# Row sums of a 64 MiB array: handing rows to the partitions at an odd distance, 111 rows in place of 112

## Chip, cores, metric

One core of a Trainium2 chip. The metric is device time in microseconds, the median of several runs.

## The reference

```python
batch, seq, dim = 32, 512, 1024
x = randn(batch, seq, dim)  as float32          # 16384 rows of 4 KiB
def reference(x, multiplier=0.5):
    return (np.sum(x, axis=-1) * multiplier).astype(np.float32)
```

67.11 MB are read, 64 KiB are written. The kernel can hardly be anything but a stream of loads with the sums beside it.

## The kernel before

Of each partition's 128 rows the first 112 are contiguous in HBM (partition p owns rows from 112p). They come in seven loads of 16 rows, 64 KiB per partition, into three buffers. The last 16 rows per partition come from the end of the array in five small pieces, so that little work is left after the last byte. VectorE sums whole blocks; ScalarE helps in the last two. The first three loads are issued ahead of the program's entry barrier.

```python
    own = rows - B                                  # 128 - 16 = 112
    x_rows = x_flat[0 : P * own, :].rearrange("(p c) d -> p c d", p=P)
    x_last = x_flat[P * own : N, :].rearrange("(p c) d -> p c d", p=P)
    x_pool = ctx.enter_context(tc.tile_pool(name="x", bufs=3))
    # ... cut ...
    for b in range(n_blocks - 1):
        c0 = b * B
        t = x_pool.tile([P, B, D], fp32, name="xb")
        loads.append(nc.sync.dma_start(out=t, in_=x_rows[:, c0 : c0 + B, :]))
        h = B if b < n_blocks - 2 else B // 2
        nc.vector.reduce_sum(out=sums[:, c0 : c0 + h], in_=t[:, 0:h, :], axis=mybir.AxisListType.X)
        # ... times mul; rows h to B on ScalarE ...
    t = x_pool.tile([P, B, D], fp32, name="xb")
    for lo, hi in [(0, 8), (8, 13), (13, 15)]:      # then row 15 in two parts
        loads.append(nc.sync.dma_start(out=t[:, lo:hi, :], in_=x_last[:, lo:hi, :]))
    early = nc.sync.dma_start(out=out_rows, in_=res[:, 0:own])
    # ... cut: row by row on VectorE and ScalarE, the last store ...
```

Of the kernel before, what the change touches and what calls it, by code (L numbers as in the profile page):

```python
# [1 line left out]

# [4 lines left out]


@with_exitstack
def kernel(  # L10
    ctx: ExitStack,
    tc: tile.TileContext,
    x: bass.AP,
    multiplier: float,
    out: bass.AP,
):










    nc = tc.nc
    P = nc.NUM_PARTITIONS
    fp32 = mybir.dt.float32
    ADD = mybir.AluOpType.add  # L30

    x_flat = x.flatten_outer_dims()
    N, D = x_flat.shape
    rows = N // P
    out_flat = out.rearrange("b s -> (b s)")
    mul = float(multiplier)

    B = 16
    n_blocks = rows // B
    assert N == P * rows and rows == n_blocks * B  # L40
    own = rows - B
    x_rows = x_flat[0 : P * own, :].rearrange("(p c) d -> p c d", p=P)
    x_last = x_flat[P * own : N, :].rearrange("(p c) d -> p c d", p=P)
    out_rows = out_flat[0 : P * own].rearrange("(p c) -> p c", p=P)
    out_last = out_flat[P * own : N].rearrange("(p c) -> p c", p=P)

    x_pool = ctx.enter_context(tc.tile_pool(name="x", bufs=3))
    res_pool = ctx.enter_context(tc.tile_pool(name="res", bufs=1))
    sums = res_pool.tile([P, rows], fp32, name="sums")
    res = res_pool.tile([P, rows], fp32, name="res")  # L50
    part = res_pool.tile([P, 1], fp32, name="part")

    SYNC = mybir.DependencyInfo(mybir.DependencyClass.Sync, mybir.DependencyReason.DATA)
    ORDER = mybir.DependencyInfo(
        mybir.DependencyClass.NoSync, mybir.DependencyReason.SCHED_ONLY
    )

    def nop_after(engine, waits_for, follows):
        i = engine.nop()
        for w in waits_for:  # L60
            tc.add_manual_dep(i.ins, w.ins.name, SYNC, reason="end seen here")
        for f in follows:
            tc.add_manual_dep(i.ins, f.ins.name, ORDER, reason="in this order")
        return i

    loads = []
    acts = []

    def act_row(t, r, col):
        acts.append(nc.scalar.activation(  # L70
            out=t[:, r, :],
            in_=t[:, r, :],
            func=mybir.ActivationFunctionType.Copy,
            scale=mul,
            accum_out=res[:, col : col + 1],
        ))

    def dve_span(t, r, lo, hi, dst, start=0.0):
        mid = (lo + hi) // 2
        return nc.vector.tensor_tensor_reduce(  # L80
            out=t[:, r, lo:mid],
            in0=t[:, r, lo:mid],
            in1=t[:, r, mid:hi],
            scale=mul,
            scalar=start,
            op0=ADD,
            op1=ADD,
            accum_out=dst,
        )

    for b in range(n_blocks - 1):
        c0 = b * B
        t = x_pool.tile([P, B, D], fp32, name="xb")
        loads.append(nc.sync.dma_start(out=t, in_=x_rows[:, c0 : c0 + B, :]))  # L94
        h = B if b < n_blocks - 2 else B // 2
        nc.vector.reduce_sum(  # L96
            out=sums[:, c0 : c0 + h], in_=t[:, 0:h, :], axis=mybir.AxisListType.X
        )
        nc.vector.tensor_single_scalar(  # L99
            out=res[:, c0 : c0 + h],  # L100
            in_=sums[:, c0 : c0 + h],
            scalar=mul,
            op=mybir.AluOpType.mult,
        )
        for r in range(h, B):
            act_row(t, r, c0 + r)

    c0 = (n_blocks - 1) * B
    t = x_pool.tile([P, B, D], fp32, name="xb")
    cut = 576  # L110
    pieces = [(0, 8), (8, 13), (13, 15)]
    for lo, hi in pieces:
        loads.append(
            nc.sync.dma_start(  # L114
                out=t[:, lo:hi, :], in_=x_last[:, lo:hi, :]
            )
        )
    for lo, hi in ((0, cut), (cut, D)):
        loads.append(
            nc.sync.dma_start(  # L120
                out=t[:, B - 1, lo:hi], in_=x_last[:, B - 1, lo:hi]
            )
        )
    early = nc.sync.dma_start(out=out_rows, in_=res[:, 0:own])
    on_act = {4, 5, 6, 7, 11, 12, 14}
    for r in range(B - 1):
        if r in on_act:
            act_row(t, r, c0 + r)
        else:
            dve_span(t, r, 0, D, res[:, c0 + r : c0 + r + 1])  # L130
    first = dve_span(t, B - 1, 0, cut, part)
    part_seen = nop_after(nc.vector, [first], [])
    final = dve_span(t, B - 1, cut, D, res[:, rows - 1 : rows], start=part)

    tc.add_manual_dep(final.ins, part_seen.ins.name, ORDER, reason="in this order")
    tc.declare_no_dep(final.ins, first.ins.name, reason="waited for by the nop in front")




    seen = nop_after(nc.sync, loads[-8:] + acts[-1:], [])
    store = nc.sync.dma_start(out=out_last, in_=res[:, own:])
    tc.add_manual_dep(store.ins, seen.ins.name, ORDER, reason="in this order")
    for a in acts[-len(on_act) :]:
        tc.declare_no_dep(store.ins, a.ins.name, reason="waited for by the nop in front")
    nop_after(nc.sync, [early, final], [store])

    def start_loads_at_entry(nc_):



        entry, *rest = nc_.main_func.blocks
        is_sp = lambda i: i.engine == mybir.EngineType.SP
        is_load = lambda i: type(i).__name__ == "InstDMACopy"
        for block in rest:
            body = list(block.instructions)
            own = [i for i in body if is_sp(i)]
            if not any(is_load(i) for i in own):
                continue
            lead = []  # L160
            for i in own:
                if not is_load(i) or i.sync_info.on_wait:
                    break
                lead.append(i)
            names = {i.name for i in lead}
            block.instructions = [i for i in body if i.name not in names]
            head = list(entry.instructions)
            at = next(
                k for k, i in enumerate(head) if is_sp(i) and type(i).__name__ == "InstDrain"
            )  # L170
            entry.instructions = head[:at] + lead + head[at:]
            return

    nc.at_finalize(start_loads_at_entry)


# [1 line left out]
_INS = ['x', 'multiplier']  # L178
_OUTS = [((32, 512), 'float32')]

_NUMBERS = {'multiplier': 0.5}


# [26 lines left out]
```

## Time and profile before

| | before |
|---|---|
| time, median of 3 runs | 162.09 us (161.96 to 162.16) |
| span of the profile | 160.2 us |
| DMA packets' share of the span | 97.4% |
| VectorE busy | 119.3 us |
| first block landed | 21.78 us |
| one block of 8 MiB in the stream | 19.35 us |

How to read it: a load has landed when what waits for its data is released; the landings given are the starts of the reductions. The time from one landing to the next is the stream's own pace. VectorE is faster than that, so whatever moves the end must act on the first landing, on the pace, or on the tail. The lines for this are in the prediction.

### The profile page before, as it was taken

To read this page: it belongs to the slowest core of one execution; us is meant where nothing else is said; L and a number is where in the kernel's file an instruction comes from. 1 tells how busy PE (TensorE), PEld (TensorE's weight loads), DVE (VectorE), ACT (ScalarE), POOL (GpSimd) and SP (SyncE) were. 2 spreads that over 40 slices of the span, in tenths; PEclk is the share of its full clock that TensorE was granted. 3 is DMA by queue.
4 is the path that set the end of the run, shared out by engine and by line. 5 is a ranking of instruction groups with operands and counts; after the bars stand their busy time and mean duration, and the time that the engine had idled before them with its cause. 6 is when DMAs were issued, how large, how long until landed. Compare 5 with 4: busy or idle time off the path is not lost.

```text
span 160.2 us, 138 instructions
## 1 busy us (share of the span) xinstructions
DVE 119.3 (74%) x34; ACT 17.3 (11%) x31; POOL 0.2 (0%) x4
## 2 busy tenths in 40 slices
DVE  0000059997799969999599995999959999597443
ACT  0000000000000000000000000000000000599952
POOL 0000000000000000000000000000000000000000
DMA  7996996996996996997997998979969969999992
GB/s 278 507 524 262 524 524 262 524 524 262 524 524 262 524 524 262 524 475 311 524 442 344 524 409 376 524 311 475 524 278 507 524 278 507 393 393 425 430 399 72
DMA packets 2016, 67.18 MB, mean 419 GB/s; under 512 B 480, under 2 KB 608, under 8 KB 736
## 3 DMA queue, kind: packets, MB, share of 16 engines
q1 hardware_dynamic: 2016, 67.18, 97.4%
HBM read 67.11 MB, written 0.07 MB: 419 GB/s over the span
## 4 chain that ended last, share of the span: by engine, by line
DMA 75%; DVE 22%; SPq 1%; issue 0%; DVEq 0%
DMA xb<-in_x_dram 75%; DVE sums L96 22%; SPq L114 1%; DVE xb L80 0%; SPq L120 0%; SPq L94 0%; DVE res L99 0%; DVEq L205 0%
## 5 line engine op out<-in xcount | busy, mean ns | idle before, releaser
L96 DVE TENSOR_REDUCE sums<-xb 128x16 f32<-128x16384 f32 (+1 forms) x7 | 112.0, 16001 | 33.3 <-DMA xb<-in_x_dram 33.3
L70 ACT ACT_TABLE_LOAD x1 | 1.3, 1283 | 137.9 <-DMA xb<-in_x_dram 137.9
L70 ACT ACTIVATE xb<-xb 128x1024 f32<-128x1024 f32 x15 | 15.7, 1045 | 2.1 <-DMA xb<-in_x_dram 2.1
L80 DVE CUSTOM_DVE_ANT_0 xb<-xb 128x512 f32<-128x512 f32 (+1 forms) x9 | 5.6, 664 | 5.0 <-DMA xb<-in_x_dram 5.0
L70 ACT ACTIVATION_READ_ACCUMULATOR xb<-xb 128x1 f32 x15 | 2.8, 187 | 0.0
L99 DVE TENSOR_SCALAR res<-sums 128x16 f32<-128x16 f32 (+1 forms) x7 | 1.2, 174 | 0.2
L80 DVE DVE_READ_ACCUMULATOR2_ANT res<- 128x1 f32 x9 | 0.7, 83 | 0.0
L80 DVE CUSTOM_DVE_ANT_0 xb<-xb,part 128x224 f32<-128x224 f32 x1 | 0.5, 450 | 0.2 <-DMA xb<-in_x_dram 0.2
L191 POOL MEMSET const-bfloat16-1.0<- 128x1 bf16 x1 | 0.1, 101 | 0.0
L191 POOL MEMSET const-uint8-127<- 128x1 uint8 x1 | 0.1, 101 | 0.0
L191 POOL MEMSET const-float32-0.0<- 128x1 f32 x1 | 0.1, 98 | 0.2 <-issue 0.2
L191 POOL MEMSET const-float32-1.0<- 128x1 f32 x1 | 0.1, 98 | 0.0
L80 DVE DVE_READ_ACCUMULATOR2_ANT part<- 128x1 f32 x1 | 0.1, 83 | 0.0
## 6 DMA issues: line engine op xcount, KB each, us to landing
xb<-in_x_dram SPq DMA_DIRECT2D x1, 4096.0 KB, 31.1
xb<-in_x_dram SPq DMA_DIRECT2D x1, 2560.0 KB, 36.9
xb<-in_x_dram SPq DMA_DIRECT2D x1, 1024.0 KB, 38.9
xb<-in_x_dram SPq DMA_DIRECT2D x1, 288.0 KB, 39.1
xb<-in_x_dram SPq DMA_DIRECT2D x1, 224.0 KB, 39.2
xb<-in_x_dram SPq DMA_DIRECT2D x7, 40.8
out_dram<-res SPq DMA_DIRECT2D x1, 56.0 KB, 10.0
out_dram<-res SPq DMA_DIRECT2D x1, 8.0 KB, 1.4
```

The lines of the kernel that those rows point to most:

```text
L70: acts.append(nc.scalar.activation(out=t[:, r, :], in_=t[:, r, :], func=mybir.ActivationFunctionType.Copy, scale=mul, accum_out=res[:, col ...
L80: return nc.vector.tensor_tensor_reduce(out=t[:, r, lo:mid], in0=t[:, r, lo:mid], in1=t[:, r, mid:hi], scale=mul, scalar=start, op0=ADD, o ...
L96: nc.vector.reduce_sum(out=sums[:, c0 : c0 + h], in_=t[:, 0:h, :], axis=mybir.AxisListType.X)
L99: nc.vector.tensor_single_scalar(out=res[:, c0 : c0 + h], in_=sums[:, c0 : c0 + h], scalar=mul, op=mybir.AluOpType.mult,)
L114: nc.sync.dma_start(out=t[:, lo:hi, :], in_=x_last[:, lo:hi, :])
L191: nc = _bacc.Bacc("TRN2", target_bir_lowering=False, num_devices=1)
```

## The change

Intent: partition 4a+b owns 111 rows from row 111(32b+a). If each engine of a load serves groups of four neighbouring partitions, the first reads of neighbouring groups then lie 111 rows apart, an odd number of 4 KiB rows, in place of 4 x 112 = 448 rows, and do not share their low address bits. With 111 rows per partition the blocks become 15 and 6 x 16 rows, and 17 rows are left for the end; the last of them gets a tile of its own (t_end), as the block's tile holds 16.

```diff
-    own = rows - B
-    x_rows = x_flat[0 : P * own, :].rearrange("(p c) d -> p c d", p=P)
+    own = rows - B - 1
+    Q = 4
+    x_rows = x_flat[0 : P * own, :].rearrange("(b a c) d -> a b c d", b=Q, c=own)
 ... (the same for out_rows)
+    c0 = 0
     for b in range(n_blocks - 1):
-        c0 = b * B
+        n = B if b else B - 1
-        loads.append(nc.sync.dma_start(out=t, in_=x_rows[:, c0 : c0 + B, :]))
+        loads.append(nc.sync.dma_start(out=t[:, 0:n, :], in_=x_rows[:, :, c0 : c0 + n, :]))
 ... 
+    t_end = res_pool.tile([P, 1, D], fp32, name="xe")
-    pieces = [(0, 8), (8, 13), (13, 15)]
+    pieces = [(0, 9), (9, 14), (14, B)]
 ... (the last row, in two parts, goes to t_end)
-    on_act = {4, 5, 6, 7, 11, 12, 14}
+    on_act = {5, 6, 7, 8, 12, 13, 15}
```

Note that the source of a load has one dimension more now (32 x 4 partitions with two different steps). I call this the split source, and the old form the plain source.

## The prediction

> **What bounds the kernel now.** I read the page first, then the chain that ended last in order of time, then the DMA bytes in stretches cut at the landings of the blocks, then the first microseconds and the tail in fine stretches. The busy shares and the chain:
>
> ```profile
> DVE 119.3 (74%) x34; ACT 17.3 (11%) x31; POOL 0.2 (0%) x4
> q1 hardware_dynamic: 2016, 67.18, 97.4%
> DMA 75%; DVE 22%; SPq 1%; issue 0%; DVEq 0%
> ...
> L96 DVE TENSOR_REDUCE sums<-xb 128x16 f32<-128x16384 f32 (+1 forms) x7 | 112.0, 16001 | 33.3 <-DMA xb<-in_x_dram 33.3
> ```
>
> VectorE waits 33.3 us for data and is busy 74%; the DMA engines' packets fill 97.4% of the span. The 22% of VectorE in the chain is no bound: it comes in where a load waits for its buffer, and the queue holds the next load by then. The stretches from one block's landing to the next show that (columns: stretch in us from the start and its length, busy us of VectorE, ScalarE and GpSimd, granted clock, DMA share, GB/s):
>
> ```profile
> 21.78:41.11 19.33, 17.39 (x2) 0.00 (x0) 0.00 (x0) 1.00 1.00 434
> 60.46:79.81 19.35, 17.39 (x3) 0.00 (x0) 0.00 (x0) 1.00 1.00 434
> 99.16:118.51 19.35, 17.39 (x2) 0.00 (x0) 0.00 (x0) 1.00 1.00 434
> 137.87:157.47 19.60, 14.48 (x20) 17.32 (x31) 0.00 (x0) 1.00 0.95 404
> 157.47:160.20 2.73, 0.46 (x2) 0.00 (x0) 0.00 (x0) 1.00 0.03 3
> ```
>
> An 8 MiB block takes 19.35 us, 8,388,608 B / 19.35 us = 433.5 GB/s, with the engines full. VectorE needs 17.39 us of each, so it has 2 us of slack. (A packet is counted where it starts, so the rows near the end read a little low; 8 MiB in the last 19.60 us is 428 GB/s.) The span is 21.78 (first landing) + 6 x 19.35 + 19.60 + 2.73 = 160.2 us. Only three places differ from the steady stream: the first block (21.78 - 19.35 = 2.43 us more), the last one (0.25 us more) and the tail of 2.73 us.
>
> The start, in tenths of a microsecond and then whole waves of 16 packets (64 KiB each, 16 x 65,536 B = 1.05 MB, which GB/s times the length of the stretch confirms):
>
> ```profile
> 1.00:1.10 0.10, 0.00 (x0) 0.00 (x0) 0.00 (x0) 1.00 7.84 2621
> 1.80:1.90 0.10, 0.00 (x0) 0.00 (x0) 0.00 (x0) 1.00 4.67 1966
> ...
> 1.00:1.95 0.95, 0.00 (x0) 0.00 (x0) 0.00 (x0) 1.00 3.03 1104
> 3.90:4.55 0.65, 0.00 (x0) 0.00 (x0) 0.00 (x0) 1.00 3.72 1613
> 8.75:9.40 0.65, 0.00 (x0) 0.00 (x0) 0.00 (x0) 1.00 3.72 1613
> ```
>
> The share counts a packet whole in the stretch where it starts, so share times length is the mean time of the wave's 16 packets: 3.03 x 0.95 = 2.88 us in the first wave, 3.72 x 0.65 = 2.42 us in the second and the fourth. In the first wave the four packets that start in 1.00 to 1.10 took 7.84 x 0.1 x 16 / 4 = 3.14 us each, the three that start in 1.80 to 1.90 took 4.67 x 0.1 x 16 / 3 = 2.49 us. So engines start over 0.9 us, the early ones are held up by about 0.7 us, and all end at nearly one time: the second wave begins within 3.90 to 4.55. After that every wave has the 2.42 us of a full stream.
>
> **What the Trainium skill says.** "DMA: Bandwidth & Descriptors", section "Latency and other measured facts", reports that HBM copies fall to half their rate when the row pitch of the partitions is a large power of two, and that 4 KiB of padding restores it; it calls the aliasing of channels an inference. Here a partition's pitch is 112 rows of 4 KiB, 448 KiB, and four partitions lie 7 x 256 KiB apart, so aliasing would fit the change's intent. The trace shows no such loss in the stream: 433.5 GB/s. The same page, section "Where 436 GB/s comes from", gives 435.2 GB/s as the ceiling of the 16 ports; the trace agrees, it stands at 99.6% of it. "The descriptor swizzle" there says that each engine of a 128-partition transfer writes one port, in groups of four neighbouring partitions, which is why the change hands out rows by 4a+b; this trace does not name engines, so it cannot confirm that.
>
> **The change part by part.**
> 1. *Rows per partition.* In lockstep the 16 engines now read 448 rows (1.75 MiB) apart, with the same low 18 address bits. Afterwards their first reads lie 111 rows or multiples apart, with different low bits. Bytes stay 67.11 MB, descriptors stay 128 per load and 64 KiB long (60 KiB in the first block). What it can remove is the hold-up of the first wave only. Mean excess is 2.88 - 2.42 = 0.46 us per engine, but the end is set by the last engine, and the late starters are the ones hardly held up: one that starts at 1.88 (the stretches place the last start just before 1.90) would end at 4.30, and the last of the second wave's starts is near 4.50. So about 0.2 us of the 0.46 can reach the end. I book it whole: -0.2 us.
> 2. *The stream.* If the odd distance also lifts 433.5 to the port ceiling of 435.2, 67.11 MB would take 154.2 in place of 154.8 us: -0.6 us at most. Nothing in the trace says that HBM is what costs the 0.4%; booked at 0.
> 3. *Block sizes.* One row of all partitions is 512 KiB, 524,288 B / 433.5 GB/s = 1.21 us. Block 0 lands 1.21 us earlier, its reduction takes 17.22 x 15/16 = 16.1 us, and all landings up to the seventh block's come 1.21 us earlier; the last 17 rows give that back. Sum 0.
> 4. *The last pieces.* The first piece has 9 rows instead of 8, five on VectorE (its rows start 0.61 us apart) and four on ScalarE (1.04 us apart). VectorE has the seventh block's half done some 1.2 us earlier, the piece lands as before near 147.5; 5 x 0.61 = 3.1 us ends near 150.6, ScalarE's 4 x 1.04 near 151.7, both before the next piece at 153.68. Later pieces have the same rows as before. Sum 0.
> 5. *Stores.* 444 and 68 B per partition in place of 448 and 64 B, no longer on multiples of 64 B. The early store takes 10.0 us to landing because it queues behind the loads, and it is no step of the chain. The last one takes 1.4 us: +0 to +0.2, booked +0.05.
> 6. *Issues.* The source has one dimension more; the first issue costs 0.38 us of SyncE now and might take 0.1 us more: +0.05 on the path, as only the first issue lies on it.
> 7. *The end tile* takes 4 KiB of a partition and no wait: its loads wait for no buffer, and before all loads had been issued by 118.7 us, far ahead of their transfer.
>
> Sum: -0.2 + 0.05 + 0.05 = -0.1; the time is 162.09 - 0.1, some 162.0 us; because part 2 can only help, I put the middle at 161.9.
>
> **The rivals.**
> *A larger gain from HBM.* If every wave paid a little for equal low bits, both part 1 in full (0.46) and part 2 (0.6) fall due: 162.09 - 1.06 = 161.0 us. For it: the early packets' 3.14 us. Against it: waves of 2.42 us from the second one on, although the engines still start within 0.65 us of each other, so if equal low bits hurt, it should have shown in each wave. The hold-up may as well be the filling of the queues, which the change leaves alone: then 162.1 us.
> *The split over the engines goes wrong.* The source's outer dimension is now 32, not 128. If the generator cuts it into 16 parts of two, an engine gets eight neighbouring partitions, hence two ports, and pairs of engines meet at one port while another is idle. The stream could fall to half, some 300 us, or less badly if the pairs drift apart. For it: nothing in the trace. Against: the change's own text counts on an odd distance of the first reads, which this split would not give (222 rows), so whoever wrote it had reason to expect groups of four. I give it 6%.
> *The stores bite.* Unaligned 68 B pieces of neighbouring partitions might cost several tenths: 162.4 us. [...]I do not expect it.
> *VectorE as the bound* is out: 17.39 of 19.35 us.
>
> **Range and chances.** What a perfect stream needs is 154.2 us at the port ceiling, plus about 1 us before the first packet, 0.5 us from last packet to landing, 2.73 us of tail and the 1.9 us between span and time: 160.3 us, an estimate from the numbers above. A gain of 2% would have to reach 158.8, below that, so its chance is 1%. Slower by 2% happens only by the second rival: 6%. Within 2%: 93%. The runs before span 0.2 us; with the first rival on the low side and stores on the high side, 161.2 to 162.5 us should hold it 8 times in 10.
>
> **What would show each step.** Right: the first wave's mean near 2.42 us and early starters ending before 4 us, the waves after it at 2.42 us as before, block 0 landing near 20.4 us, later landings 19.35 us apart, the seventh near 136.5, the last load's near 157.3, span near 160.0. Wrong in part 1: a first wave still at 2.88 us means queue filling, not addresses. Wrong in part 2: landings 19.28 us apart. The second rival would show as packets of more than 2.5 us in every wave, and a stream below 420 GB/s; a slow store as more than 1.6 us to landing.

## The result

| | before | after |
|---|---|---|
| time, median of 6 runs | 162.10 us | 163.02 us |
| lowest and highest | 161.96 to 162.18 | 162.92 to 163.11 |
| span | 160.2 us | 161.2 us |
| first block landed | 21.78 us (16 rows) | 21.59 us (15 rows) |

The ratio is 1.0056, interval 1.0043 to 1.0069: 0.9 us slower, clear of noise, but inside 2%. (Ratios are the mean time of one kernel's fast runs over that of the other's of the same rounds, so they are not quite the ratios of the medians.) The prediction had a gain, 161.9 us, and 162.5 us as the top of its range.

Where the time went shows in the same stretches as before, cut at the landings of the changed kernel (columns as in the prediction: stretch, length, busy us of VectorE, ScalarE, GpSimd, clock, DMA share, GB/s):

```profile
21.59:40.94 19.35, 16.33 (x3) 0.00 (x0) 0.00 (x0) 1.00 1.00 434
60.29:79.64 19.35, 17.39 (x2) 0.00 (x0) 0.00 (x0) 1.00 1.00 434
98.99:118.34 19.35, 17.40 (x3) 0.00 (x0) 0.00 (x0) 1.00 1.00 434
```

The stream is what it was, 19.35 us for a block of 16 rows. The seventh block landed at 137.69 us and the last reduction began at 158.54 us, 20.85 us later; before it was 137.87 and 157.55, 19.68 us, and one row more (1.21 us) makes 20.89. After that both need 2.7 us. So nothing is lost after the first block. But the first block had one row less and should have landed 1.21 us earlier, at 20.57; it landed at 21.59. **All of the loss, 1.02 us, is in the first load.** Its beginning in the chain of work that ended last, in order of time (start us, length us, what; SPq is SyncE's queue, which issues the load), of before:

```profile
0.00 0.38 SPq L94
0.38 0.05 issue
0.43 40.66 DMA xb<-in_x_dram
```

and after:

```profile
0.00 0.65 SPq L97
0.65 0.05 issue
0.70 40.21 DMA xb<-in_x_dram
```

The first issue takes 0.27 us longer. The rest lies between it and the end of the first wave of 16 packets. The stretches where packets start, before (the first row is the first wave, the next ones the starts of the second wave):

```profile
0.90:2.50 1.60, 0.00 (x0) 0.00 (x0) 0.00 (x0) 1.00 1.80 655
3.80:4.20 0.40, 0.00 (x0) 0.00 (x0) 0.00 (x0) 1.00 1.13 492
4.20:4.60 0.40, 0.00 (x0) 0.00 (x0) 0.00 (x0) 1.00 4.91 2130
4.60:5.00 0.40, 0.00 (x0) 0.00 (x0) 0.00 (x0) 1.00 0.00 0
```

and after, with the first wave in a narrower stretch too, and three more rows from 130 us later:

```profile
0.90:2.50 1.60, 0.00 (x0) 0.00 (x0) 0.00 (x0) 1.00 1.92 614
1.40:2.10 0.70, 0.00 (x0) 0.00 (x0) 0.00 (x0) 1.00 4.38 1404
4.20:4.60 0.40, 0.00 (x0) 0.00 (x0) 0.00 (x0) 1.00 3.20 1382
4.60:5.00 0.40, 0.00 (x0) 0.00 (x0) 0.00 (x0) 1.00 1.77 768
5.00:5.40 0.40, 0.00 (x0) 0.00 (x0) 0.00 (x0) 1.00 0.71 307
...
136.10:136.50 0.40, 0.00 (x0) 0.00 (x0) 0.00 (x0) 1.00 1.93 830
136.50:136.90 0.40, 0.00 (x0) 0.00 (x0) 0.00 (x0) 1.00 1.07 461
136.90:137.30 0.40, 0.00 (x0) 0.00 (x0) 0.00 (x0) 1.00 0.43 184
```

GB/s times length over the packet's size counts the packets that start in a stretch. Before (64 KiB), 492 x 0.4 / 65.5 = 3 engines begin their second packet in 3.80 to 4.20 us and 13 in 4.20 to 4.60. After (60 KiB, which would take 0.15 us less), 9 begin it in 4.20 to 4.60, 5 in 4.60 to 5.00 and 2 only in 5.00 to 5.40. All 16 first packets begin within 1.40 to 2.10 us, where before's began within 1.00 to 1.95: the change starts 0.4 us later, and then its engines come apart. The first wave's mean packet, 1.92 x 1.6 = 3.07 us in place of 2.88, is no measure of the loss: a run without loss, with the same packets (e5 below), has it too:

```profile
0.90:2.50 1.60, 0.00 (x0) 0.00 (x0) 0.00 (x0) 1.00 1.92 614
```

What counts is the last engine. Cut into hundredths, the stretches put the last second packet's start at 4.50 us before and at 5.37 after. In all 14 profiles with whole 64 KiB first packets, of before and of the experiments below, the first block lands 17.27 to 17.31 us after that start (4.50 and 21.78 before, 4.85 and 22.13 in e4, 5.24 and 22.51 in e3, 5.60 and 22.87 in e1), and in the five with 60 KiB 16.20 to 16.24 us after it (5.37 and 21.59 in the change). At 136 us the 36 KiB packets of the last block start 9, 5 and 2 to a stretch again. The trace names no engine, but both fit an engine that stays as late as it came out of its first packet, and a load that has landed only when its last engine is done. So two stragglers in the first packet cost the whole kernel their delay.

### The profile page after: what moved, and what is told of

Read it like the earlier page. It is cut to its first block, busy times and chain, and to the rows that moved or that the text cites. A ratio compares the mean times of both kernels' runs of the same rounds, so it can differ in the third digit from the quotient of the medians.

```text
span 161.2 us, 140 instructions
## 1 busy us (share of the span) xinstructions
DVE 118.9 (74%) x36; ACT 17.3 (11%) x31; POOL 0.2 (0%) x4
## 4 chain that ended last, share of the span: by engine, by line
DMA 75%; DVE 22%; SPq 1%; issue 0%; DVEq 0%
DMA xb<-in_x_dram 50%; DMA xe<-in_x_dram 25%; DVE sums L99 21%; SPq L117 1%; DVE xe L82 1%; SPq L97 0%; DVE res L102 0%; DVEq L61 0%; DVE part L82 0%; DVEq L201 0%
## 5 line engine op out<-in xcount | busy, mean ns | idle before, releaser
L99 DVE TENSOR_REDUCE sums<-xb 128x16 f32<-128x16384 f32 (+2 forms) x7 | 110.9, 15848 | 34.2 <-DMA xb<-in_x_dram 34.2
L82 DVE CUSTOM_DVE_ANT_0 xb<-xb 128x512 f32<-128x512 f32 x9 | 5.8, 689 | 5.5 <-DMA xb<-in_x_dram 5.5
L102 DVE TENSOR_SCALAR res<-sums 128x16 f32<-128x16 f32 (+2 forms) x7 | 1.2, 174 | 0.2
L82 DVE CUSTOM_DVE_ANT_0 xe<-xe,part 128x224 f32<-128x224 f32 x1 | 0.5, 450 | 0.2 <-DMA xe<-in_x_dram 0.2
L82 DVE CUSTOM_DVE_ANT_0 xe<-xe 128x288 f32<-128x288 f32 x1 | 0.5, 458 | 0.0
## 6 DMA issues: line engine op xcount, KB each, us to landing
out_dram<-res SPq DMA_DIRECT2D x1, 55.5 KB, 11.2
```

The costliest lines, as they stand in the source:

```text
L82: return nc.vector.tensor_tensor_reduce(out=t[:, r, lo:mid], in0=t[:, r, lo:mid], in1=t[:, r, mid:hi], scale=mul, scalar=start, op0=ADD, o ...
L102: nc.vector.tensor_single_scalar(out=res[:, c0 : c0 + h], in_=sums[:, c0 : c0 + h], scalar=mul, op=mybir.AluOpType.mult,)
```

## The experiments

Question: is it the form of the source, where the first packets read, or the 15-row block? All runs had five rounds against before on the same chip; e1 to e4, e5 to e8, e9 to e12, f1 to f4, and g1 with g2 were on a chip each. "Wrong on purpose" means that some partitions got other rows than they should, with the same bytes moved. Pitch is the distance from one partition's first row to the next one's. Landing is the first block's in the run's one profile, whose own time may be off the median (e1's was its slowest run, 163.19 us, f1's and f2's their fastest); one with 15 rows is brought to 16 by adding 1.21 us, in brackets.

| run | what differs from before | median us | ratio (95% interval) | first landing us |
|---|---|---|---|---|
| e1_map_112 | split source, 112 rows apart, all loads | 162.86 | 1.0050 (1.0037 to 1.0062) | 22.87 |
| e2_rows_111 | blocks of the change, plain, 444 apart | 162.41 | 1.0025 (1.0012 to 1.0037) | (22.48) |
| e3_plain_near | first load plain, 111 apart | 162.62 | 1.0032 (1.0019 to 1.0044) | 22.51 |
| e4_split_far | first load split, 448 apart | 162.45 | 1.0024 (1.0011 to 1.0038) | 22.13 |
| e5_pitch_112 | blocks of the change, plain, 448 apart | 162.16 | 0.9999 (0.9987 to 1.0012) | (21.86) |
| e6_first_444 | first load plain, 444 apart | 162.39 | 1.0015 (1.0002 to 1.0029) | 22.17 |
| e7_first_64 | first load plain, 64 apart | 162.15 | 1.0000 (0.9987 to 1.0012) | 21.98 |
| e8_first_65 | first load plain, 65 apart | 162.10 | 0.9997 (0.9984 to 1.0009) | 21.78 |
| e9_lead_one | loads 2 and 3 issued after the barrier | 162.15 | 0.9999 (0.9985 to 1.0013) | 21.78 |
| e10_one_row_first | first load cut into 1 and 15 rows | 162.31 | 1.0011 (0.9999 to 1.0024) | 21.95 |
| e11_near_shifted | as e3, addresses 37 rows up | 162.19 | 1.0009 (0.9996 to 1.0021) | 21.96 |
| e12_undo_first | the change, first load plain, 448 apart | 162.19 | 1.0009 (0.9997 to 1.0022) | (21.86) |
| f1_near_again | e3 repeated | 162.73 | 1.0037 (1.0025 to 1.0050) | 22.27 |
| f2_near_64up | as e3, 64 rows up | 162.59 | 1.0026 (1.0014 to 1.0039) | 22.12 |
| f3_after_37up | the change, first load 37 rows up | 162.72 | 1.0040 (1.0028 to 1.0053) | (22.45) |
| f4_far_37up | first load plain, 448 apart, 37 rows up | 162.12 | 1.0001 (0.9988 to 1.0015) | 21.79 |
| g1_first_113 | first load plain, 113 apart | 162.39 | 1.0016 (1.0003 to 1.0030) | 22.28 |
| g2_near_37_again | e11 repeated | 162.28 | 1.0009 (0.9997 to 1.0022) | 22.04 |

The "apart" column of the table counts from the first partition of one group of four to that of the next; that an engine serves such groups is what the Trainium skill states ("DMA: Bandwidth & Descriptors", section "The descriptor swizzle"), not visible in a trace. By its formula the engines' first groups are numbers 0 to 7 and 16 to 23, so between the two halves the first reads lie nine such distances apart.

**First four: form against addresses against sizes.**

e1, the new hand-out with the old number of rows:
```diff
-    x_rows = x_flat[0 : P * own, :].rearrange("(p c) d -> p c d", p=P)
+    x_rows = x_flat[0 : P * own, :].rearrange("(b a c) d -> a b c d", b=4, c=own)
```

> The rows of before (112 per partition, blocks of 16), but handed out by 4a+b, so every load but the last has the split source, and first reads of the engines lie 112 rows (an even number) apart. Form theory (the split source makes the issue 0.2 us longer and starts the first wave late and uneven): first landing near 22.8 us in place of 21.78, time near 163.0 us, ratio to before about 1.006. Address theory (it is the distance of the first reads that matters, and 111 rows are worse than 448): 112 rows share other low bits than 111, so a time unlike that of the change, and most likely 162.1 plus the 0.2 us of the issue. Size theory (the 60 KiB packets of a 15-row first block are at fault): 162.1 to 162.3.

e2, the new number of rows with the old hand-out:
```diff
-    x_rows = x_flat[0 : P * own, :].rearrange("(b a c) d -> a b c d", b=Q, c=own)
+    x_rows = x_flat[0 : P * own, :].rearrange("(p c) d -> p c d", p=P)
```

> The blocks of the change (111 rows, 15 first, 17 last, own tile for the last row), but partition p owns rows from 111p as before: plain source, engines 444 rows apart. Form theory: no loss, first landing near 20.6 us, time 162.1, ratio 1.000. Address theory: 444 rows are 4 times odd, between the two; 162.1 to 162.6. Size theory: the full loss, 163.0.

e3 and e4 alter only the first load of before. e3 takes the change's first-read distance with a plain source (27.75 rows per partition, so 111 per four), e4 the split source with the old distance:
```diff
+        if b == 0:                                   # e3
+            E = 28416                                # 27.75 rows of 1024
+            src = x_flat.rearrange("n d -> (n d)")[0 : P * E].rearrange("(p e) -> p e", e=E)
+            loads.append(nc.sync.dma_start(out=t.rearrange("p b d -> p (b d)"), in_=src[:, 0 : B * D]))
```
```diff
+        if b == 0:                                   # e4
+            src = x_flat[0 : 32 * 448, :].rearrange("(a q) d -> a q d", q=448)
+            src = src[:, 0 : 4 * 111, :].rearrange("a (b c) d -> a b c d", b=4)
+            loads.append(nc.sync.dma_start(out=t, in_=src[:, :, 0:B, :]))
```

> Wrong result on purpose in the first block: before, with only the first load reading at a pitch of 27.75 rows per partition, so that the engines' first reads lie exactly 111 rows apart as in the change, with a plain source (one step for the partitions). Form theory: issue 0.38 us, first landing near 21.8, time 162.1, ratio 1.000. Address theory: the full loss, first landing near 22.6, time 162.9.

> Wrong result on purpose in the first block: before, with only the first load's source split into 32 x 4 (steps of 448 and 111 rows), so that the engines' first reads lie 448 rows apart as in before. Form theory: issue 0.65 us, first landing near 22.8, time 163.0, ratio 1.006. Address theory: only the issue's 0.2 to 0.3 us, time 162.3 to 162.4.

Measured: every theory that wanted to be the only cause falls. The form alone costs 0.36 us (e4), the near first reads alone 0.53 us (e3); together 0.89, and the change lost 0.92. (e3 has the change's rows only where a group of four begins; its other partitions read elsewhere. So the sum is a good fit, not a proof.) The two look different in the profile. The first stretches of e4:

```profile
0.90:2.50 1.60, 0.00 (x0) 0.00 (x0) 0.00 (x0) 1.00 1.95 655
4.20:4.60 0.40, 0.00 (x0) 0.00 (x0) 0.00 (x0) 1.00 1.51 655
4.60:5.00 0.40, 0.00 (x0) 0.00 (x0) 0.00 (x0) 1.00 4.54 1966
5.00:5.40 0.40, 0.00 (x0) 0.00 (x0) 0.00 (x0) 1.00 0.00 0
```

Second packets start 4 and 12 to a stretch, a group as close as before's (3 and 13) and 0.4 us later: the split source delays all engines alike. Its first packets already begin at 1.41 us in place of 1.01, so the form costs its time before the first packet, not in the first wave. The issues themselves (durations min/median/max in ns) of before and of the change:

```profile
L94 SPq DMA_DIRECT2D xb<-in_x_dram x7: 327/328/432, 0.0 to 97.1; - x7
```
```profile
L97 SPq DMA_DIRECT2D xb<-in_x_dram x7: 535/535/654, 0.0 to 96.9; - x7
```

An issue of a split source takes 207 ns longer, and only the first one stands in the path; there the chain shows 0.65 in place of 0.38 us, 0.27 of the 0.36. In e4 it took 0.64, and the first packet began 0.77 us after it in place of 0.63. The first stretches of e3:

```profile
0.90:2.50 1.60, 0.00 (x0) 0.00 (x0) 0.00 (x0) 1.00 2.02 655
3.80:4.20 0.40, 0.00 (x0) 0.00 (x0) 0.00 (x0) 1.00 1.13 492
4.20:4.60 0.40, 0.00 (x0) 0.00 (x0) 0.00 (x0) 1.00 3.41 1475
4.60:5.00 0.40, 0.00 (x0) 0.00 (x0) 0.00 (x0) 1.00 1.13 492
5.00:5.40 0.40, 0.00 (x0) 0.00 (x0) 0.00 (x0) 1.00 0.38 164
```

3, 9, 3 and 1: most engines come out as in before, four late, one in 5.00 to 5.40. The near reads do not delay all, they make stragglers. How many varies: in the profile of f1, the same kernel again, three were late and none started after 5.00. e1, split and 112 rows apart, lost 0.8 us, 0.4 more than the form alone (112 rows with a plain source was not run); e2, plain at 444 rows, lost 0.3.

**Second four: sizes and distances.** e5 is e2 with the pitch put back to 112 rows; e6, e7 and e8 are e3 with another E:
```diff
-    x_rows = x_flat[0 : P * own, :].rearrange("(p c) d -> p c d", p=P)          # e5
+    x_rows = x_flat[0 : P * (own + 1), :].rearrange("(p c) d -> p c d", p=P)
```
```diff
-            E = 28416
+            E = 111 * 1024        # e6: 444 rows;  e7: 16 * 1024, 64 rows;  e8: 16 * 1024 + 256, 65 rows
```

> Wrong result on purpose: the blocks of the change (15 rows first, 17 last, own tile), plain source, but the pitch of the partitions back at 112 rows, so the engines' first reads lie 448 rows apart. Size theory for the 0.3 us that the run with 444 rows lost (the 15-row first block or the 17-row end costs it): 162.4. Address theory (448 rows, a multiple of 64 rows, is a good distance and 444 is not): 162.1.

> Wrong result on purpose in the first block: before, with only the first load at a pitch of 111 rows, engines 444 rows apart, blocks of 16. Address theory: 162.4 to 162.5, first landing near 22.2. Size theory: 162.1, landing 21.8.

> Wrong result on purpose in the first block: before, with only the first load at a pitch of 16 rows, so its 8 MiB are one stretch and the engines' first reads lie 64 rows (256 KiB) apart. If what helps is a distance that is a multiple of 64 rows: 162.1, landing 21.8. If what helps is reading far apart (the span of addresses): a loss as at 111 rows or more, 162.6 or above.

> Wrong result on purpose in the first block: the same with a pitch of 16.25 rows, engines' first reads 65 rows apart, nearly the same span of addresses. Multiple-of-64 theory: slower than the 64-row run by 0.3 to 0.6 us. Span theory: equal to it. The intent of the change (odd distances spread the first reads best): faster than it.

e5 clears the block sizes, the pieces, the last row's own tile and the stores of 68 B: 162.16 us. e6 shows that 444 rows alone cost 0.24. I then thought that a multiple of 64 rows is what makes a distance good (448 is one, 444, 112 and 111 are not). e7 fits that, but e8 refutes it: 65 rows, odd, cost nothing. They gain nothing either, which is against the change's intent.

**Third four: whose cost, and can it be lowered?** e12 is the change with its first load alone undone; e11 is e3 moved up by 37 rows; e9 and e10 alter before to see what the hold-up of its first wave is:
```diff
+        if b == 0:                                                               # e12
+            src = x_flat[0 : P * (own + 1), :].rearrange("(p c) d -> p c d", p=P)[:, 0:n, :]
```
```diff
-            src = x_flat.rearrange("n d -> (n d)")[0 : P * E]...                  # e11
+            src = x_flat.rearrange("n d -> (n d)")[37 * D : 37 * D + P * E]...
```
```diff
+            lead = lead[:1]                       # e9: only the first load goes ahead of the barrier
```
```diff
+        for lo, hi in ((0, 1), (1, B)) if b == 0 else ((0, B),):                  # e10
+            loads.append(nc.sync.dma_start(out=t[:, lo:hi, :], in_=x_rows[:, c0 + lo : c0 + hi, :]))
```

> Wrong result on purpose in the first block: the change, with its first load alone (15 rows) given the plain source at a pitch of 112 rows again; the other six loads keep the split source and 111 rows. If all of the loss arises in the first load's first packets: 162.1, first landing near 20.65. If later loads carry part of it: above 162.3.

> Wrong result on purpose in the first block: the run with first reads 111 rows apart and a plain source, with all its addresses moved up by 37 rows. If the distances alone decide: 162.6 as before the move. If the loss belongs to certain addresses (which rows the engines hit): another time, most likely nearer 162.1.

> Before, with only the first load issued ahead of the entry's barrier and the second and third in the body. If the hold-up of the first wave (mean packet 2.88 us against 2.42) comes from the descriptors of the second and third load being made at that time, the first wave's mean packet falls towards 2.42 and the first landing comes 0.2 to 0.8 us earlier, time 161.3 to 161.9. If it is a start-up cost of the first load's own reads: no change, 162.1.

> Before, with the first load cut into its first row (4 KiB packets) and the other 15. If the hold-up is a fixed start cost that every engine pays once, the 4 KiB packets carry it and the time stays at 162.1 (up to 0.2 us more for the one issue more). If it grows with the bytes of the first packet (64 KiB from each of 16 places at once), it shrinks: 161.6 to 161.9.

e12: with six loads still split and 111 rows apart, the time is 162.19 us. One of its five runs took 162.62, the others 162.10 to 162.19. So the loss belongs to the first load, as the landings said; later loads' longer issues hide behind the queue. Its second packets all start before 4.60 us, 9 in the first stretch and 7 in the second:

```profile
3.80:4.20 0.40, 0.00 (x0) 0.00 (x0) 0.00 (x0) 1.00 3.19 1382
4.20:4.60 0.40, 0.00 (x0) 0.00 (x0) 0.00 (x0) 1.00 2.48 1075
4.60:5.00 0.40, 0.00 (x0) 0.00 (x0) 0.00 (x0) 1.00 0.00 0
```

e11: the same distances at other addresses, and most of the loss is gone. Its second packets start 5, 9 and 2 to a stretch, and the two late ones at 4.65 and 4.67 us:

```profile
3.80:4.20 0.40, 0.00 (x0) 0.00 (x0) 0.00 (x0) 1.00 1.89 819
4.20:4.60 0.40, 0.00 (x0) 0.00 (x0) 0.00 (x0) 1.00 3.40 1475
4.60:5.00 0.40, 0.00 (x0) 0.00 (x0) 0.00 (x0) 1.00 0.76 328
```

e9 changed nothing, with the same landing at 21.78 us, but it does not settle whether the next loads' descriptors hold up the first wave. Its issues of loads 2 and 3 only moved from 0.43 to 1.33 us to this, still in the first wave:

```profile
0.80 0.81 SPq L94 DMA_DIRECT2D xb<-in_x_dram  x2
```

e10 refutes that the hold-up shrinks with smaller first packets; it is 0.2 us slower if anything, and its interval includes 1.

**Last six: distance or addresses?** f1 and g2 repeat e3 and e11 unchanged. f2, f3 and f4 move the first load of e3, of the change and of before, and g1 is another odd distance:
```diff
-            ...[37 * D : 37 * D + P * E]                       # f2, against e11
+            ...[64 * D : 64 * D + P * E]
```
```diff
+            src = x_flat[37 : 37 + P * own, :].rearrange("(b a c) d -> a b c d", b=Q, c=own)   # f3, first load
```
```diff
+            src = x_flat[37 : 37 + P * own, :].rearrange("(p c) d -> p c d", p=P)              # f4, first load
```
```diff
-            E = 28416
+            E = 28928                                          # g1: 28.25 rows, 113 per four
```

> The plain first load with first reads 111 rows apart once more, unchanged (wrong result on purpose in the first block), as a control. If addresses decide: 162.6 again. If the first finding was the chip's: 162.2.

> The same with all addresses of the first load 64 rows (256 KiB) higher (wrong result on purpose). If the low 18 bits of the addresses decide: 162.6 as without the move. If higher bits matter too: another time, between 162.1 and 162.6.

> The change with its first load 37 rows higher (wrong result on purpose in the first block), split source and 111 rows kept. If the addresses' part goes and the split's part stays: 162.4 to 162.5. If the distances decide after all: 163.0. If the move helps by chance of the plain form alone: anything between.

> Before with its first load 37 rows higher (wrong result on purpose in the first block), plain source, 448 rows apart. If before has good distances: 162.1. If before only has good addresses: 162.3 to 162.6.

> Before, with only the first load at a plain pitch of 28.25 rows, first reads 113 rows apart (wrong result on purpose in the first block). If a spacing near 110 rows loses whatever the addresses: 162.6. If it is a matter of which addresses meet: any time from 162.1 to 162.7, so a time under 162.3 would show that 111 is not bad for being odd.

> The first load 111 rows apart and 37 rows higher, once more unchanged (wrong result on purpose). If the first finding holds: 162.2. If it was the job: 162.6.

Both repeats, on other chips, agree with their first runs (1.0032 and 1.0037; 1.0009 and 1.0009): the ten runs of e3 and f1 lie at 162.51 to 162.88 us, the ten of e11 and g2 at 162.15 to 162.40. The two places were never run on one chip, so that the chip plays a part is spoken against only by f3 (the moved place on f1's chip) and by each side having two chips that agree. At 111 rows the loss is 0.5 to 0.6 us in place, 0.46 us 64 rows up and some 0.1 us 37 rows up: the distance alone does not decide, the addresses do. f3 agrees: moved up, the change lost 0.6 in place of 0.9 us, near the form's 0.36 plus the 0.1 that e11 and g2 kept (but its interval is 0.45 to 0.86, and that of the change begins at 0.70). f2, at 162.59, came out as its expectation had it if the low 18 bits of the addresses decide: a move by 64 rows leaves these bits as they are, one by 37 rows does not. Its interval overlaps f1's. f4 stays at 162.12, so before does not sit on lucky rows; 448 rows held at both places tried. g1 loses 0.24 us: another odd distance, another size of loss. That is above the 162.3 us set before the run, so g1 does not clear odd distances; e8 does. No version beat the kernel before.

What stays open: which property of the addresses makes some first packets take up to a microsecond longer. The trace does not name the engine of a packet or the part of the memory it reads. Equal low 18 bits (448 and 64 rows) never cost anything here, and 65 rows did not either, so neither a rule by shared low bits nor one by oddness fits. That the loss depends on which low 18 bits meet is still possible: f2 fits it, and no run was made to refute it. Nor is it known what the hold-up of about 0.7 us is that all the plain kernels' early engines share.

## Why the prediction was wrong

1. *Rows per partition (booked -0.2 us): this is the step that failed, in sign.* It took the hold-up of the first wave for something that the addresses cause, and that other addresses would therefore remove. The runs show two separate things. Nothing that was tried lessened the common hold-up, neither other addresses nor 4 KiB first packets (e4, e5, e7, e8, e10: none is faster than before; e9 hardly moved the next loads' issues). Nor was the mean of 2.88 us, from which the 0.46 us came, a measure of it: before, e8, e9 and f4 have means of 2.88, 3.06, 3.15 and 3.02 us, and in all four the last second packet starts at 4.49 to 4.51 us. The addresses act on single engines, as stragglers, and the change's addresses made them, where before had next to none: +0.53 to +0.60 us (e3, f1). The prediction did see that the last engine sets the end. It asked only how much the last one could gain, not how a new last one could arise.
2. *The stream (booked 0): right.* 19.35 us per block before and after. It had little room, at 99.6% of the port ceiling that the prediction takes from the Trainium skill, and the six later loads at 111 rows and in split form cost nothing (e12).
3. *Block sizes (0) and 4. the last pieces (0): right.* e5 has them all at 162.16 us, and the last 17 rows took 20.85 us against 20.89 by the sum. The landings forecast at 20.4, 136.5 and 157.3 us came at 21.59, 137.69 and 158.39: late by the first load's miss and by no more.
5. *Stores (+0.05): harmless.* The last one took 1.4 us to landing before and after, and e5 bears it out. The early one took 11.2 in place of 10.0 us, off the chain.
6. *Issues (+0.05): right in kind, mis-sized.* The first issue took 0.27 us more where I allowed for up to 0.1; with the later begin of the first packet after it, it is 0.36 us (e4).
7. *The end tile: no wait appeared.* e5 has it too.

In sum, +0.36 for the form and +0.53 to +0.60 for the addresses, 0.89 to 0.96 us, where the change lost 0.92. So the forecast missed by the 0.2 us of gain that did not come, by the stragglers, and by 0.3 us of the form's cost. Of the rivals, the larger gain from HBM did not come. The worst one, engines in pairs on one port, did not either: the stream stood at 434 GB/s. The rival of slow stores has no share. That the change leaves the hold-up alone, as the rival of "the filling of the queues" had it, was right; that the filling is its cause is not shown. The prediction's sign for that, a first wave still at 2.88 us, could not tell the cases apart, as the means above show. A rival that the first wave could get worse was missing.

## What to carry to other kernels

When a stream of loads runs at its ceiling, only its start and its end are left, and here the slowest of the 16 engines counted, not their mean: look at when the engines begin their second packet, because here the same spread was still there 130 us later. Keep the very first load in its simplest form, since its issue was the one that nothing hid (e4, e12), and give an unusual hand-out of rows to the later loads if they need it. Before changing addresses against a suspected conflict, ask whether the trace shows the conflict in the stream; a first wave that is slow is no evidence for it.

## What the Trainium skill lacked or had wrong

- "DMA: Bandwidth & Descriptors", section "Latency and other measured facts", has the loss at pitches of large powers of two in HBM copies and 4 KiB of padding as its cure. For a 448 KiB pitch, which is not such a power, no run shows a loss (433.5 GB/s), and an odd number of 4 KiB rows between the first reads cured nothing: 0.0 us at 65 rows, +0.24 at 113, +0.5 to +0.6 at 111. No page has the loss seen here, of 0.5 to 0.6 us in a load's first packets alone, or that moving all its addresses by 37 rows leaves some 0.1 us of it.
- The same page gives a first-byte latency of about 0.6 us for this path (section "Specifications"), which fits 0.38 us of issue and first packets in 1.00 to 1.10. It lacks that the first wave's 64 KiB packets took 2.88 to 3.2 us on the mean in these runs, against 2.42 in the stream.
- No page has the cost of one more step in the source of a load: 535 against 328 ns per issue, 0.65 against 0.38 us for the first.
- No page says that the spread of the engines after their first packets lasts: 9, 5 and 2 packets start in three successive stretches of 0.4 us at 4.2 us and again at 136.1 us, and the first landing follows the last of the second packets' starts by 17.27 to 17.31 us.
